# Weight operands of the second feed-forward half made during the first half and kept in DRAM

## The chip, the cores and the metric

The kernel runs on one core of one Trainium2 chip. The time is device microseconds of one execution. TensorE (PE) does the matmuls, VectorE (DVE), ScalarE (ACT) and GpSimd (POOL) the rest, SyncE (SP) issues most DMAs; POOL issues some of its own. SBUF is on the chip, PSUM holds what TensorE accumulates, DRAM is outside.

## The reference, cut to what matters

An encoder block on x (1024 tokens x 1024 columns, float32): attention with a pooling branch, a norm, and a feed-forward network whose hidden width is 2816. Only the last part is touched:

```python
h = modulate(layer_norm(x), sh2, sc2)
gt, up = jnp.split(h @ w_ffn_in[l], 2, axis=-1)
y = (jax.nn.silu(gt) * up) @ w_ffn_out[l]
x = layer_norm(ALPHA * x + g2[:, None, :] * y, ln2_g[l], ln2_b[l])
```

## The kernel before

Float32 products are made of three matmuls. `split` turns an operand into a high half (`hi`, a cast on ACT) and a low half (`lo` = operand - `hi`, a subtract on DVE), and `mm3` (lines 98 to 101) adds high x high, high x low and low x high in PSUM. Both halves of the feed-forward network are 2x2 block products in Winograd's form: seven products of blocks in place of eight, whose operands are blocks or sums and differences of blocks.

The **first half** (lines 1164 to 1179) runs over 22 pairs of column tiles (gate and up). A pair is seven products of 12 matmuls, 84 in all, into the PSUM tiles `fa` and `fb`. For each pair SP loads `rg` and `ru` (512 KB each); `rest_w` forms the sums of weights (POOL lines 973 and 979, DVE lines 975 and 980) and splits them into `oh`, `ol`. Between the products stand copies out of PSUM: `first_cp` copies `p1`, `rest_a` copies `u2` and `p5` (ACT, lines 1058 and 1061); DVE adds at lines 933, 1068 and 1070; the activation follows (lines 1074 to 1076), and two tiles `th` of 128 x 512 are stored to `midD` in DRAM by SP. Products accumulate on the same PSUM tiles, so a copy has to be done before the next product on its tile starts; TensorE works on the other tile meanwhile. The order on each engine is that of a scheduler here, except for the first pairs.

The **second half** (lines 1182 to 1440) multiplies the hidden activations, read back from `midD` into the blocks `m11`, `m12`, `m21`, `m22` (11 tiles of 128 x 512 each; `m11` lies in the tile `mA`, `m21` in `mB`), with the blocks of `w_ffn_out`. The order of all engines is written out by hand. Products go in the order q = 2, 1, 5, 6, 3, 7, 4, each in 11 steps k, and a step is 12 matmuls into four PSUM tiles `oa` or `ob`. Ahead of step i the program text puts: `loads` of weights six steps ahead (SP, 512 KB for two steps, into the three buffers of `raw`), `sums` four steps ahead and `splits` three steps ahead. `sums` forms the sums of activations on POOL (lines 1234, 1237, 1241, 1244) and the sums of weights: `wx` (POOL line 1231, DVE line 1238), line 1245 on POOL, and `t4_sum` (POOL line 1338, for product 4, whose weights `t4_load` brings into `mB`). `splits` splits both operands of a step: the activations to `moh`, `mol` (four buffers), the weights to `wo` (buffers `whi`, `wlo`, two each). The last two steps of product 7 and the last four of product 4 (`late`) are run per PSUM tile at the product's end, so that the tiles finish one after the other.

Between the steps stand `hooks`: POOL's loads of blocks (`chunk`, line 1331), the loads of the residual x1 from `x1D`, `zl` and `zr` (DVE lines 1269 and 1270: the residual of the first four row tiles), `zn` and `zo` (ACT's norm and, by `gain_pool`, POOL lines 1284 and 1285: gain and bias of the output, then the store to the output), and `c22` (residual and statistics for the last four row tiles, DVE lines 1269, 1270, 1307). `evac` empties the PSUM tiles at the end of each product.

Of the kernel before, what the change touches and what calls it, by code (L numbers as in the profile page):

```python
# [9 lines left out]
F32 = mybir.dt.float32  # L10
# [8 lines left out]
P = 128  # L19
# [16 lines left out]
def encoder_block_kernel(  # L36
# [37 lines left out]
    midD = dram.tile([2, NF, P, HF], F32, tag="midD", name="midD")  # L74

# [85 lines left out]
    # mod columns: GEMV of rows [128 k x 1024] accumulated on DVE, reduced over partitions by PE  # L161
# [40 lines left out]
    batch = [("u", 3, 3072 + 3 * P), ("u", 2, 3072 + 2 * P), ("q", 0, 0)]  # L202
    wb = {}
    with tc.tile_pool(name="pre", bufs=1, reuse_waits="tile") as pre:
# [99 lines left out]
        def batch_mm(g0, n0=0, n1=6, step=1):  # L304
            """The first products with the contraction outermost, as the tiles of h arrive."""
# [21 lines left out]
        def distances(i):  # L327
            """Half of the table of -|key - query|."""
# [82 lines left out]
        # lambda  # L411
# [69 lines left out]
    with ExitStack() as ctx2:  # L481
# [39 lines left out]
        # ---- pooling branch, with the projections of head 0  # L521
# [191 lines left out]
        # remaining modulation vectors  # L713
# [243 lines left out]
    def rest_w(f, rawg, rawu, step):  # L957
        """Operands (gate, up columns) of the last five products of pair f: their sums and splits."""
# [224 lines left out]
    # Token halves, halves of the hidden channels and column halves form 2x2 blocks again;  # L1183
    # the sums of blocks replace blocks that no later product reads.
    mA = big.tile([P, 16, HF], F32, tag="A", name="mA")
    mB = big.tile([P, 16, HF], F32, tag="B", name="mB")
    with tc.tile_pool(name="fo", bufs=1, reuse_waits="tile") as fo:
# [5 lines left out]
        wx = fo.tile([P, NK, HF], F32, name="wx")  # L1193
# [12 lines left out]
        raws, ops, src = {}, {(2, k): out_ops[k] for k in range(2)}, {}  # L1206

        def wload(q, p, i, j):
            n = min(2, NK - p)
            r = wp.tile([P, 2, HF], F32, tag="raw", bufs=3, name="w%d_%d" % (q, p))  # L1210
            nc.sync.dma_start(r[:, 0:n, :], wblock(i, j, p, n))
            raws[q, p] = r[:, 0:n, :]

        WSRC = {2: (1, 0), 1: (0, 0), 6: (1, 1), 3: (1, 1), 7: (0, 0)}
# [255 lines left out]
```

## Time and profile before

| | |
|---|---|
| median of 3 runs | 1675.31 us (1674.59 to 1677.12) |
| span of the profiled execution (the only time given for it) | 1677.4 us |
| PE busy | 1578.5 us, 94% |
| DVE busy | 1189.5 us, 71% |
| ACT busy | 709.9 us, 42% |
| POOL busy | 421.7 us, 25% |
| DMA over the span | 190.76 MB, 114 GB/s |

The profile is of one execution, so a sum made from its rows gives a time against 1677.4 us; the median of the runs is 2.1 us below that. The feed-forward network's first half ends and its second half starts at about 1401 us; the last matmul ends near 1660.8 us, and the output's last tiles follow. Shares of the whole span say little about either half; the rows further down are of stretches of them.

### The profile page before, as it was taken

The page shows a single profiled execution, that of the slowest core. Times are in us where ns is not written, and L with a number is a line of the kernel's source. Part 1 is how long each engine was busy: PE and PEld are TensorE (multiplying, and loading weights), DVE is VectorE, ACT ScalarE, POOL GpSimd, SP SyncE. Part 2 cuts the span into 40 slices and gives each one's busy share as a digit, 9 for nine tenths or more (in the row PEclk, how much of TensorE's full clock was granted, in tenths as well). Part 3 has the DMA queues.
Part 4 walks back from the last instruction along what each step waited for, and adds up shares of the span by engine and source line. Part 5 has one row for each costly group of instructions (what it writes and reads, how often), then busy time and mean ns, then how long its engine had stood idle before and what let it go on. Part 6 is the DMA issues. An engine that isn't in the chain of part 4 may idle for free.

```text
span 1677.4 us, 20367 instructions
## 1 busy us (share of the span) xinstructions
PE 1578.5 (94%) x7634; PEld 1308.7 (78%) x7634; DVE 1189.5 (71%) x1664; ACT 709.9 (42%) x1228; POOL 421.7 (25%) x382
## 2 busy tenths in 40 slices
PE   5899999999999999999989979999999999969874
PEld 3787888888888888888878757888888888858653
DVE  7676868685966667675657896555555554898998
ACT  3445545454545545454532444333333334425341
POOL 4300001010102101000142471212111111574793
PEclk8999999999999999999999989999999999989997
DMA  9244334151433323213063513322322228724321
GB/s 332 60 122 145 105 95 132 45 150 64 133 94 101 120 82 119 57 57 101 27 224 131 170 51 100 97 80 78 99 76 86 77 89 290 255 76 150 107 107 63
DMA packets 169333, 190.76 MB, mean 114 GB/s; under 512 B 7185, under 2 KB 125010, under 8 KB 169234
## 3 DMA queue, kind: packets, MB, share of 16 engines
q1 hardware_dynamic: 165392, 176.06, 33.6%
q0 software_dynamic: 3184, 12.32, 2.0%
q8 instruction: 60, 0.98, 0.2%
q10 hardware_dynamic: 658, 1.08, 0.2%
q14 instruction: 39, 0.32, 0.1%
HBM read 144.34 MB, written 36.70 MB: 108 GB/s over the span
## 4 chain that ended last, share of the span: by engine, by line
PE 75%; DVE 14%; issue 4%; DMA 3%; POOL 3%; ACT 1%; SPq 0%; DVEq 0%; POOLq 0%; ACTq 0%
PE fa L99 4%; PE fa L100 4%; PE fa L101 4%; PE fb L99 3%; PE fb L100 3%; PE fb L101 3%; PE at L651 3%; PE s L628 3%; PE s L630 3%; DVE wo L96 2%; PE pp L99 2%; PE pp L100 2%; PE pp L101 2%; PE pv L99 2%; PE pv L100 2%
## 5 line engine op out<-in xcount | busy, mean ns | idle before, releaser
L637 ACT ACTIVATE e<-e,nm 128x1024 f32<-128x1024 f32 x128 | 147.1, 1150 | 111.1 <-DVE nm L635 109.8
L635 DVE CUSTOM_DVE_ANT_0 e<-s,table 128x1024 f32<-128x1024 f32 x128 | 153.1, 1217 | 24.9 <-PE s L630 24.4
L96 DVE TENSOR_TENSOR ol<-ws,oh 128x512 fp32r<-128x512 f32 x88 | 61.0, 695 | 76.4 <-ACT oh L95 76.3
L628 PE MATMUL s<-k,q 128*128 128x512 f32 x256 | 105.3, 411 | 1.2 <-DVE nm L635 1.2
L96 DVE TENSOR_TENSOR al<-at,ah 128x512 fp32r<-128x512 f32 x128 | 83.2, 684 | 31.9 <-ACT ah L95 31.4
L979 POOL TENSOR_TENSOR ws<-rg,ru 128x512 f32<-128x512 f32 x22 | 45.7, 2075 | 228.1 <-DVE ol L96 217.2
L630 PE MATMUL s<-k,q 128*128 128x512 f32 x256 | 101.5, 397 | 0.0
L95 ACT CAST oh<-ws 128x512 fp32r<-128x512 f32 x88 | 53.9, 616 | 104.4 <-POOL ws L979 66.7
L642 DVE SCALAR_TENSOR_TENSOR e<-e,c,e 128x1024 f32<-128x1024 f32 x64 | 87.4, 1365 | 1.9
L100 PE MATMUL oa<-wo,moh 128*128 128x512 f32 x176 | 73.0, 415 | 15.3 <-DVE wo L96 15.3
L95 ACT CAST ah<-at 128x512 fp32r<-128x512 f32 x128 | 70.0, 596 | 25.1 <-PE at L651 25.1
L99 PE MATMUL oa<-wo,moh 128*128 128x512 f32 x176 | 71.6, 407 | 3.3 <-ACT wo L95 3.3
L651 PE MATMUL at<-ident,e 128*128 128x128 f32 x512 | 68.9, 275 | 6.0 <-DVE e L642 3.2
L99 PE MATMUL av<-ah,vh 128*128 128x256 f32 x256 | 73.9, 289 | 0.3 <-ACT ah L95 0.2
L99 PE MATMUL fa<-oA,oh 128*128 128x512 f32 x176 | 69.8, 397 | 2.9 <-ACT oh L95 2.7
L101 PE MATMUL av<-ah,vl 128*128 128x256 f32 x256 | 72.6, 284 | 0.0
L100 PE MATMUL av<-al,vh 128*128 128x256 f32 x256 | 72.5, 283 | 0.0
L101 PE MATMUL oa<-wo,mol 128*128 128x512 f32 x176 | 71.9, 408 | 0.0
L101 PE MATMUL fa<-oA,ol 128*128 128x512 f32 x176 | 69.7, 396 | 1.1 <-DVE ol L96 1.0
L100 PE MATMUL fa<-oA,oh 128*128 128x512 f32 x176 | 69.6, 396 | 0.5 <-DVE oA L1051 0.5
L681 POOL TENSOR_TENSOR rm_1v<-rm_1s,rm_1v 128x4 f32<-128x4 f32 x8 | 5.0, 624 | 251.8 <-ACT rm_1s L672 251.8
L651 PEld LDWEIGHTS at<-ident,e 128*128 128x128 f32 x512 | 58.7, 144 | 11.7 <-DVE e L642 3.6
(562 smaller groups left out, 4812.3 us busy)
## 6 DMA issues: line engine op xcount, KB each, us to landing
ada<-in_w_ada_dram SPq DMA_DIRECT2D x32, 512.0 KB, 3.8
rg<-in_w_ffn_in_dram SPq DMA_DIRECT2D x26, 512.0 KB, 3.9
w<-in_w_ffn_out_dram SPq DMA_DIRECT2D x24, 512.0 KB, 3.9
ru<-in_w_ffn_in_dram SPq DMA_DIRECT2D x22, 512.0 KB, 3.8
midD<-th SPq DMA_DIRECT2D x42, 256.0 KB, 2.1
q<-q SPq DMA_DIRECT2D x32, 256.0 KB, 2.9
mt<-mixD SPq DMA_DIRECT2D x12, 448.0 KB, 6.4
x<-in_x_dram SPq DMA_DIRECT2D x8, 512.0 KB, 6.3
```

The costliest lines, as they stand in the source:

```text
L95: nc.scalar.copy(hi, src)
L96: (eng or nc.vector).tensor_tensor(lo, src, hi.bitcast(F32), op=ALU.subtract)
L99: nc.tensor.matmul(ps, lh, rh, start=start, stop=False, skip_group_check=skip)
L100: nc.tensor.matmul(ps, lh, rl, start=False, stop=False, skip_group_check=skip)
L101: nc.tensor.matmul(ps, ll, rh, start=False, stop=stop, skip_group_check=skip)
L628: nc.tensor.matmul(ps[:, cs], q[:, 0, jj * P:(jj + 1) * P], kd[h, m][:, cs], start=True, stop=False)
L630: nc.tensor.matmul(ps[:, cs], q[:, 1, jj * P:(jj + 1) * P], kd[h, m][:, cs], start=False, stop=True)
L635: nc.vector.tensor_tensor_reduce(out=t, in0=ps, in1=table[:, o0:o0 + S], scale=-slope, scalar=3.0e38, op0=ALU.add, op1=ALU.min, accum_out=nm)
L637: nc.scalar.activation(t, t, AF.Exp, bias=nm, scale=-1.0, accum_out=zt[:, m, j:j + 1])
L642: nc.vector.scalar_tensor_tensor(s[1], s[1], c1, s[0], op0=ALU.mult, op1=ALU.add)
L651: nc.tensor.matmul(pt[:, i, :], a[:, kt * P:(kt + 1) * P], ident, start=True, stop=True, is_transpose=True)
L979: pol(sa, r11, r21, op=ALU.subtract)
```

## The change

A new DRAM tile `wfD` holds, for each of the seven products and each k, a finished weight operand: both halves of a tile, 128 partitions x 2 x 512, 512 KB, 4 KB in a row per partition.

`fw_prep`, a generator, makes them in the first half. For each k it loads the four blocks of `w_ffn_out` (256 KB each, one buffer each), splits the seven operands into tiles `fwo` (two buffers; ACT's cast, DVE's subtract), stores each with a DMA on SP, and forms the sums between by four POOL subtractions. The loop over pairs draws eight pieces of it for every k, spread over the pairs from the second on. In all: 44 loads, 77 casts, 77 subtracts on DVE, 44 on POOL, 77 stores.

In the second half the weights' loads, sums and splits go, and so do `wx`, `t4_load` and `t4_sum`. `fw_load` reads a step's operand from `wfD` into a ring of seven buffers (the ones that `raw`, `whi` and `wlo` had), still six steps ahead. At the end of products 7 and 4 the loads, like the splits, now stand behind the late blocks. TensorE's rows are the same 6817 in the same order.

```diff
+    RING = ("whi", "wlo", "raw", "whi", "wlo", "raw", "raw")
+    def fw_load(q, k):
+        tag = RING[nring[0] % len(RING)]
+        nring[0] += 1
+        w = wp.tile([P, 2, HF], F32R, tag=tag, bufs=3 if tag == "raw" else 2, name="w%d_%d" % (q, k))
+        nc.sync.dma_start(w.bitcast(F32), wfD[q - 1, k])
+        return w
...
+    def fw_prep():
+        def op(q, k, src):
+            w = fwp.tile([P, 2, HF], F32R, tag="fwo", bufs=2, name="fw%d_%d" % (q, k))
+            split(w[:, 0, :], w[:, 1, :], src)
+            nc.sync.dma_start(wfD[q - 1, k], w.bitcast(F32))
+        for k in range(NK):
+            w11, w12, w21, w22 = [fwp.tile([P, HF], F32, tag="fw%d%d" % ij, bufs=1, name="fw%d%d_%d" % (*ij, k))
+                                  for ij in ((0, 0), (0, 1), (1, 0), (1, 1))]
...
+            op(2, k, w21)
+            pol(w12, w12, w11, op=ALU.subtract)
+            yield
+            op(3, k, w22)
+            pol(w22, w22, w12, op=ALU.subtract)
+            yield
+            op(1, k, w11)
+            pol(w11, w22, w11, op=ALU.subtract)
...
+            op(5, k, w12)
+            pol(w21, w21, w22, op=ALU.subtract)
...
         if f == 0:
             hrs.close()
+            fwp = hp.enter_context(tc.tile_pool(name="fwp", bufs=1, side="right", reuse_waits="tile"))
+            prep = fw_prep()
+        else:
+            for _ in range(8 * NK * f // (NF - 2) - 8 * NK * (f - 1) // (NF - 2)):
+                next(prep, None)
...
         def loads(q, k):
-            if k % 2 == 0 and q in WSRC:
-                wload(q, k, *WSRC[q])
+            ws[q, k] = fw_load(q, k)
...
             elif q == 1:
-                pol(x, x, w, op=ALU.subtract)
-                r = m11_, w
+                r = m11_
...
             split(m[0], m[1], src[q, k][0])
-            split(w[:, 0, :], w[:, 1, :], src[q, k][1])
-            ops[q, k] = (m, w)
+            ops[q, k] = (m, ws[q, k])
...
-                        if fn is splits and n and k == NK - 1:
-                            behind.append(steps[i + ahead])
+                        if fn is not sums and n and k == NK - 1:
+                            behind.append((fn, steps[i + ahead]))
```

ACT in the first half, pair 12, from the cast of its fourth operand to the copy `p5`. Before:

```order
L95 CAST oh12_3_10239<-ws12_1_10222 128x512
L928 COPY p1_12_10218<-fa12_10192 128x512
L1074 ACTIVATE th12_0_10313<-p1_12_10218 128x512
L95 CAST oh12_4_10243<-ru12_10186 128x512
L1058 COPY u2_12_10259<-fa12_10192 128x512
L95 CAST oh13_0_10364<-ws13_1_10361 128x512
L1061 COPY p5_12_10273<-fb12_10193 128x512
```

Now; `fw<q>_<k>` is the operand of product q, step k, and `fw00` to `fw11` are the four blocks:

```order
L96 CAST oh12_3_10483<-ws12_1_10466 128x512
L96 CAST fw2_8_11072<-fw10_8_11066 128x512
L96 CAST fw3_8_11216<-fw11_8_11067 128x512
L929 COPY p1_12_10462<-fa12_10436 128x512
L96 CAST fw1_8_11221<-fw00_8_11064 128x512
L1075 ACTIVATE th12_0_10557<-p1_12_10462 128x512
L96 CAST fw5_8_11226<-fw01_8_11065 128x512
L96 CAST oh12_4_10487<-ru12_10430 128x512
L1059 COPY u2_12_10503<-fa12_10436 128x512
L96 CAST fw6_8_11231<-fw11_8_11067 128x512
L1062 COPY p5_12_10517<-fb12_10437 128x512
```

The scheduler put five casts of `fw_prep` among these rows, two directly ahead of the copy `p1` and one directly ahead of `p5`; over the whole half it packs `fw_prep` into pairs 1 to 15 and leaves pairs 16 to 21 without.

POOL at the start of the second half, from its first load there (`m12`, `mA`, `mB`, `m22` are the blocks of activations). Before:

```order
L1331 DMA m12_11601<-midD_76 128x512
L1331 DMA mA_11596<-midD_76 128x4x512
L1416 DMA wx_11604<-in_w_ffn_out_dram 128x4x512
L1331 DMA mA_11596<-midD_76 128x7x512
L1416 DMA wx_11604<-in_w_ffn_out_dram 128x7x512
L1231 TENSOR_TENSOR wx_11604<-wx_11604,w1_0_11744 128x1024
L1231 TENSOR_TENSOR wx_11604<-wx_11604,w1_2_11784 128x1024
L1231 TENSOR_TENSOR wx_11604<-wx_11604,w1_4_11825 128x1024
L1331 DMA mB_11597<-midD_76 128x4x512
L1331 DMA m22_11605<-midD_76 128x4x512
L1231 TENSOR_TENSOR wx_11604<-wx_11604,w1_6_11870 128x1024
L1231 TENSOR_TENSOR wx_11604<-wx_11604,w1_8_11913 128x1024
```

Now:

```order
L1359 DMA m12_12042<-midD_76 128x512
L1359 DMA mA_12037<-midD_76 128x4x512
L1359 DMA mA_12037<-midD_76 128x7x512
L1359 DMA mB_12038<-midD_76 128x4x512
L1359 DMA m22_12045<-midD_76 128x4x512
L1359 DMA mB_12038<-midD_76 128x7x512
L1359 DMA m22_12045<-midD_76 128x7x512
L1269 TENSOR_TENSOR mB_12038<-mB_12038,m22_12045 128x1024 x5
L1269 TENSOR_TENSOR mB_12038<-mB_12038,m22_12045 128x512
```

The loads of `wx` and its sums (line 1231) are gone, and with them what stood between the loads: seven loads of activations follow one another.

DVE in product 4, from the split of step 4 to that of step 5, with one `c22` between. Before:

```order
L96 TENSOR_TENSOR mol4_4_13150<-m22_11605,moh4_4_13149 128x512
L96 TENSOR_TENSOR wo4_4_13151<-mB_11597,wo4_4_13151 128x512
L1269 TENSOR_TENSOR m12_11601<-m12_11601,mA_11596 128x512
L1270 SCALAR_TENSOR_TENSOR m12_11601<-mA_11596,m12_11601 128x512
L1307 BN_STATS e3_11603<-m12_11601 128x6
L96 TENSOR_TENSOR mol4_5_13172<-m22_11605,moh4_5_13171 128x512
L96 TENSOR_TENSOR wo4_5_13173<-mB_11597,wo4_5_13173 128x512
```

Now:

```order
L97 TENSOR_TENSOR mol4_4_13439<-m22_12045,moh4_4_13438 128x512
L1297 TENSOR_TENSOR m12_12042<-m12_12042,mA_12037 128x512
L1298 SCALAR_TENSOR_TENSOR m12_12042<-mA_12037,m12_12042 128x512
L1335 BN_STATS e3_12044<-m12_12042 128x6
L97 TENSOR_TENSOR mol4_5_13460<-m22_12045,moh4_5_13459 128x512
```

The subtract for the weights (`wo`) is gone from each step; that of the activations (`mol`) and the three rows of `c22` stay.

## Rows read from the trace of the kernel before

**Rows 1.** Windows: busy us (and instructions) by engine, granted clock, DMA

```profile
core 0: us, PE busy (x) PEld busy (x) DVE busy (x) ACT busy (x) POOL busy (x), PEclk, DMA share, GB/s
1067.00:1401.00 334.00, 333.91 (x1473) 276.49 (x1474) 181.55 (x263) 118.39 (x196) 57.32 (x33) 1.00 0.29 93
...
1474.00:1510.00 36.00, 23.05 (x86) 17.86 (x85) 35.86 (x27) 8.23 (x16) 24.22 (x10) 0.86 0.28 89
...
1548.00:1599.60 51.60, 45.30 (x191) 36.29 (x189) 48.55 (x45) 16.43 (x28) 39.22 (x20) 0.97 0.37 117
1599.60:1660.80 61.20, 47.48 (x170) 35.39 (x168) 57.29 (x66) 19.47 (x31) 38.03 (x30) 0.89 0.19 70
```

**Rows 2.** TensorE's waits in the second half: us in total, times, longest

```profile
PE oa L100 <- DVE wo L96: 15.3, 8, 4.9
PE ob L100 <- DVE wo L96: 14.4, 4, 8.0
...
PE oa L99 <- ACT wo L95: 3.3, 2, 2.1
```

**Rows 3.** Timeline of POOL: start us, us, engine, line, operation

```profile
1474.31 15.56 POOL L1237 TENSOR_TENSOR mA<-mB,mA 128x1024 f32<-128x1024 f32 x6
```

**Rows 4.** Timeline of DVE: in A, at B's dense stretch, in C

```profile
1485.91 2.82 DVE L96 TENSOR_TENSOR wo<-wx,wo 128x512 fp32r<-128x512 f32 x1
...
1576.69 2.47 DVE L1378 TENSOR_TENSOR zlo<-zlo,ob 128x512 f32<-128x512 f32 x4
...
1617.08 2.88 DVE L96 TENSOR_TENSOR wo<-mB,wo 128x512 fp32r<-128x512 f32 x1
...
1650.05 0.68 DVE L96 TENSOR_TENSOR wo<-mB,wo 128x512 fp32r<-128x512 f32 x1
```

**Rows 5.** Groups, second half: busy us, mean ns | idle before, releaser

```profile
L96 DVE TENSOR_TENSOR wo<-w,wo 128x512 fp32r<-128x512 f32 x42 | 47.3, 1127 | 1.5 <-ACT wo L95 1.2
...
L1338 POOL TENSOR_TENSOR mB<-mB,wx 128x512 f32<-128x512 f32 x11 | 18.3, 1678 | 34.6 <-DMA mB<-in_w_ffn_out_dram 34.6
...
L1245 POOL TENSOR_TENSOR w<-wx,w 128x1024 f32<-128x1024 f32 (+1 forms) x6 | 14.5, 2410 | 6.8 <-DMA w<-in_w_ffn_out_dram 6.8
...
L1231 POOL TENSOR_TENSOR wx<-wx,w 128x1024 f32<-128x1024 f32 (+1 forms) x6 | 13.7, 2296 | 23.5 <-DMA w<-in_w_ffn_out_dram 23.5
...
L1284 POOL TENSOR_TENSOR zlo<-zlo,mA 128x1024 f32<-128x1024 f32 x4 | 10.9, 2728 | 0.0
L1285 POOL TENSOR_TENSOR zlo<-zlo,mB 128x1024 f32<-128x1024 f32 x4 | 10.8, 2702 | 0.3
```

**Rows 6.** Groups, first half, 1067 to 1401: same columns

```profile
L96 DVE TENSOR_TENSOR ol<-ws,oh 128x512 fp32r<-128x512 f32 x68 | 46.9, 690 | 63.1 <-ACT oh L95 63.1
L95 ACT CAST oh<-ws 128x512 fp32r<-128x512 f32 x68 | 41.9, 616 | 81.2 <-POOL ws L979 51.1 <-PE fb L100 27.3 <-PE fa L100 2.8
...
L973 POOL TENSOR_TENSOR ws<-ru 128x512 f32<-128x512 f32 x16 | 20.7, 1291 | 63.3 <-DVE ol L96 39.4 <-DMA ru<-in_w_ffn_in_dram 23.9
...
L1068 DVE TENSOR_TENSOR p<-p,fa 128x512 f32<-128x512 f32 x18 | 12.4, 688 | 16.8 <-PE fa L101 16.8
...
L1058 ACT COPY u<-fa 128x512 f32<-128x512 f32 x18 | 10.4, 579 | 0.0
```

**Rows 7.** DMA from 1412 to 1424: packets, MB, share; us to landing

```profile
DMA packets 1403, 4.64 MB, mean 386 GB/s; under 512 B 80, under 2 KB 80, under 8 KB 1402
...
q0 software_dynamic: 986, 3.84, 83.9%
q1 hardware_dynamic: 416, 0.79, 18.1%
...
w<-in_w_ffn_out_dram SPq DMA_DIRECT2D x3, 512.0 KB, 9.1
```

**Rows 8.** DMA issues of the whole run: KB each, us to landing

```profile
x1D<-zx SPq DMA_DIRECT2D x4, 512.0 KB, 2.6
```

More of the change, by code (lines that the diff above doesn't have):

```diff
@@ L1144, in encoder_block_kernel @@
     NK = NF // 2
-    def wblock(i, j, p, n):
-        return wfo[(i * NK + p) * P:(i * NK + p + n) * P, j * HF:(j + 1) * HF].rearrange("(f p) c -> p f c", p=P)
+    RING = ("whi", "wlo", "raw", "whi", "wlo", "raw", "raw")
+    nring = [0]
+    def fw_load(q, k):
[4 more added lines that the diff above has]
+        return w
     def first_out():
-        m, w = [wp.tile([P, 2, HF], F32, tag="raw", bufs=3, name="raw_" + nm) for nm in ("m", "w")]
+        ws = [fw_load(2, k) for k in range(2)]
+        m = wp.tile([P, 2, HF], F32, tag="raw", bufs=3, name="raw_m")
+        nring[0] += 1
         nc.sync.dma_start(m, midD[0, NK:NK + 2].rearrange("f p c -> p f c"))
-        nc.sync.dma_start(w, wblock(1, 0, 0, 2))
         ops = []
@@ L1157, in first_out @@
                   for tag in ("oh", "ol")]
-            wo_ = wp.tile([P, 2, HF], F32R, tag=("whi", "wlo")[k], bufs=2, name="w_%d" % k)
             split(mo[0], mo[1], m[:, k, :])
-            split(wo_[:, 0, :], wo_[:, 1, :], w[:, k, :])
-            ops.append((mo, wo_))
-        return ops
+            ops.append((mo, ws[k]))
+        return ops
+    def fw_prep():
[6 more added lines that the diff above has]
+                                  for ij in ((0, 0), (0, 1), (1, 0), (1, 1))]
+            for w, i, j in ((w11, 0, 0), (w12, 0, 1), (w21, 1, 0), (w22, 1, 1)):
+                nc.sync.dma_start(w, wfo[(i * NK + k) * P:(i * NK + k + 1) * P, j * HF:(j + 1) * HF])
+            yield
[4 more added lines that the diff above has]
+            pol(w22, w22, w12, op=ALU.subtract)
+            yield
+            op(1, k, w11)
+            pol(w11, w22, w11, op=ALU.subtract)
+            yield
+            op(5, k, w12)
+            pol(w21, w21, w22, op=ALU.subtract)
+            yield
+            op(6, k, w22)
+            yield
+            op(7, k, w11)
+            yield
+            op(4, k, w21)
+            yield
     for f in range(NF):
@@ L1204, in encoder_block_kernel @@
             b += [s_[:, 0:HF], s_[:, HF:]]
[L1206 to L1214, printed above, removed]
+        ops, src = {(2, k): out_ops[k] for k in range(2)}, {}
+        ws = {}
         def loads(q, k):
-            if k % 2 == 0 and q in WSRC:
-                wload(q, k, *WSRC[q])
+            ws[q, k] = fw_load(q, k)
         def sums(q, k):
@@ L1224, in sums @@
             n = min(2, NK - k)
[L1225 to L1227 removed]
+            m11_, m12_, m21_, m22_ = [m[:, k:k + n, :] for m in (m11, m12, m21, m22)]
             if q == 2:
[L1229 removed]
+                r = m12_
             elif q == 1:
[L1231 to L1232 removed]
+                r = m11_
             elif q == 5:
                 pol(m21_, m21_, m22_, op=ALU.add)
[L1235 removed]
+                r = m21_
             elif q == 6:
                 pol(m11_, m21_, m11_, op=ALU.subtract)
[L1238 to L1239 removed]
+                r = m11_
             elif q == 3:
                 pol(m12_, m12_, m11_, op=ALU.subtract)
[L1242 removed]
+                r = m12_
             elif q == 7:
                 pol(m11_, m22_, m11_, op=ALU.subtract)
[L1245 to L1246 removed]
+                r = m11_
             else:
[L1248 removed]
+                r = m22_
             for i in range(n):
[L1250 to L1252 removed]
+                src[q, k + i] = r[:, i, :]
         def splits(q, k):
@@ L1331, in chunk @@
             q.dma_start(dst[:, p:e, :], midD[half, k0 + p:k0 + e].rearrange("f p c -> p f c"))
-        def t4_load():
-            for p, e in ((0, 4), (4, NK)):
-                nc.sync.dma_start(m21[:, p:e, :], wblock(1, 0, p, e - p))
-        def t4_sum(k):
-            pol(m21[:, k, :], m21[:, k, :], wx[:, k, :], op=ALU.subtract)
         xh = [xr[:, 0:HF], xr[:, HF:]]
@@ L1362, in encoder_block_kernel @@
             hook(*((7, 9), (4, 0), (4, 2), (4, 4))[t], zo, t)
-        hook(6, NK - 1, t4_load)
-        for k in range(NK):
-            hook(3, k, t4_sum, k)
         def evac(q, t):
@@ L1415, in encoder_block_kernel @@
                 chunk(m11, 0, 0, p, e, nc.gpsimd)
-                nc.gpsimd.dma_start(wx[:, p:e, :], wblock(0, 1, p, e - p))
             for i in range(-6, len(steps)):
@@ L1438, in encoder_block_kernel @@
                         evac(q, t)
-                    for step in behind:
-                        splits(*step)
+                    for fn, step in behind:
+                        fn(*step)
 _INS = ['x', 'c', 'w_ada', 'b_ada', 'w_in', 'lambda_q1', 'lambda_k1', 'lambda_q2', 'lambda_k2', 'sub_g',
```

19 lines of the change are left out of this document (2 added, 17 removed).

## The prediction

> **What bounds the kernel now.** The table of windows comes first [rows 1], since the two halves of the feed-forward network have different limits. In the first half TensorE is never idle: 1473 matmuls in 334.00 us, 0.2267 us each, clock 1.00, VectorE (DVE) busy for 181.55 us of the 334. There only TensorE sets the time. The second half needs 7 x 132 = 924 matmuls, 209.5 us at that rate, and takes 258.97 us (1401.80 to 1660.77): 49 us are lost. By the same rows, length less matmuls x 0.2267:
> A, 1474 to 1510: 36.0 - 86 x 0.2267 = 16.5 us. B, 1548 to 1599.6: 51.6 - 191 x 0.2267 = 8.3 us. C, 1599.6 to 1660.8: 61.2 - 170 x 0.2267 = 22.7 us. In A and C the granted clock is below 1 (0.86, 0.89), so part of the loss is matmuls that ran slower after a gap.
>
> The list of TensorE's waits tells for whom it waits: 15.3 + 14.4 us for the low half of a weight operand (`wo`, DVE), 3.3 us for its high half [rows 2]. The timelines of GpSimd (POOL) and DVE tell why that is late: in A POOL runs sums without a pause, six of 1024 columns in 15.56 us [rows 3], and in that time one DVE subtract of 512 columns with both operands in SBUF takes 2.82 us [rows 4], against 0.69 us on average in the first half [rows 6]. With four operations of 2.47 us together (0.62 each) DVE reading PSUM is spared at such a time [rows 4]. So while POOL is dense, DVE does about one subtract per 2.8 us. A step of TensorE (12 matmuls) lasts 2.72 us and now asks for two subtracts, one for the activations, one for the weights: 5.6 us. That is the loss.
>
> **What the change takes out of the second half.** 77 casts on ScalarE (ACT), 77 `wo` subtracts on DVE (42 of them are the first of [rows 5]), six more sums on DVE, and on POOL the sums of weights: 18.3 + 14.5 + 13.7 = 46.5 us [rows 5]. TensorE's work and order stay. One subtract per step is left: 2.8 us against 2.72 at POOL's densest, about even.
>
> A: what could remain is the residuals of product 5 (two DVE operations every second step), if POOL is still dense there: nine operations x 2.8 = 25 us in five steps (13.6 us), less three steps of operands in hand (8 us), 3 us. From 0 (POOL done earlier: its activations load sooner) to 8 us. I take 2: **gain 14.5 us**.
>
> B: the stretch has 39.22 us of POOL work in 51.6 us; without the sums of line 1338 and most of line 1245, no dense run covers two steps. I leave 1 of 8.3 (0.5 to 3): **gain 7.3 us**.
>
> C: the end is set by the last `wo` at 1650.05 [rows 4], behind which the sixteen late blocks of product 4 run (48 matmuls, 10.9 us, to 1661). DVE's queue to that point passes POOL's run of the output gain, 10.9 + 10.8 = 21.7 us [rows 5], which stays, and which leaves DVE eight places of 2.8 us whatever stands in them. Nine `wo` fewer (11 in product 4, two done before the run) shorten the queue behind the run by 9 x 0.65 = 5.9 us. The 3.3 us of waits for the high half [rows 2] stand just before the run; they go, but SP's queue holds the x1 loads of the residuals behind operand loads now, so I count 2.5 of them. Bounds: 3 us (only those waits), 13 us (product 4 at 132 x 0.2267 = 29.9 us from its start at 1617). **Gain 8.4 us.**
>
> **What it adds at the seam.** The start of the second half now puts all loads of the POOL queue in a row: 33 blocks of 256 KB for the hidden activations and one in advance, 8.9 MB with no sum between. Before, such loads drew 3.84 MB in 12 us, 320 GB/s, while SP's queue got 0.79 MB, 66 GB/s, and a weight load of 512 KB took 9.1 us to land [rows 7]. At 320 GB/s 8.9 MB take 28 us, 10.3 steps. Each step needs 512 KB; five are in hand (loads run six steps ahead), and 66 GB/s x 28 us brings 3.5 more: 8.5 of 10.3, so 1.8 steps, 5 us, are lost. The other end is zero. SP's packets there were 0.79 MB / 416 = 1.9 KB; the finished pairs are read in rows of 4 KB. If SP's queue keeps its count of packets it gets 132 GB/s, 7 loads, and nothing is late. I take the measured rate: **loss 5 us**, since that row is of the same two queues.
>
> The Trainium skill, page "DMA: Bandwidth & Descriptors", section "Queues, rings and completion order", says that each DMA engine turns between the queues that have work, a packet from each. By that the two queues would share some 386 GB/s evenly, 193 GB/s for SP, just what a step of 2.72 us draws, and the sum would be 5 us better (R4 below). The counts (986 packets against 416 in this window) don't show an even turn, though nothing there says that SP's queue always had work.
>
> **What it adds to the first half.** 44 loads, 77 casts, 77 DVE subtracts, 44 POOL subtracts and 77 stores of 512 KB (40 MB), packed by the order into pairs 1 to 15: 5.1 operands a pair, whose length is 84 matmuls, 19.0 us. Per pair:
> DVE: 181.55 / 17.6 pairs = 10.3 us, plus 5.1 x 0.69 = 3.5, plus up to 2.9 POOL sums x 1.29 us [rows 6] during which DVE may stand, 3.8: 17.6 of 19.0. ACT: 118.39 / 17.6 = 6.7, plus 5.1 x 0.62 = 3.2: 9.9. DMA: 93 GB/s, plus 51 MB / 285 us = 179: 272 GB/s, under the 386 that a full window showed [rows 7]. Nothing is over its limit, so the bound from below is zero.
>
> But order costs. The new operand has two buffers, so a cast waits for the store two operands earlier. Such a turn is cast 0.62, subtract 0.69 [rows 6], some 0.4 to issue, and a landing of 2.6 us [rows 8] to 4 (my estimate beside other traffic): 4.3 to 5.7 us. 5.1 operands through two buffers take 11 to 14.5 us of 19. They fit, but not at any moment: ACT's order puts such casts directly ahead of the copies `p1`, `u2` and `p5`. The next product but one overwrites what they read, so each has a product of 2.72 us less its own 0.58 [rows 6], 2.1 us, to be late. The same holds of DVE's line 1068, which TensorE needs one product later and which now can meet a POOL sum. A cast that arrives a turn too early can stand 1 to 4 us, past that room. I take 0.6 us a pair, 15 pairs: **loss 9 us** (0 to 28, the end at 1.9 us a pair, one full late turn less the room).
>
> **Sum.** 14.5 + 7.3 + 8.4 - 5 - 9 = 16.2 us. The profiled execution's span is 1677.4 us; 1661.2 follows, and the median of the runs is 2.1 us below the span: **1659 us**.
>
> **Rivals.**
> R1, slower: the two-buffer ring bounds the first half. It decides when a turn passes 8.2 us, since 5.1 x 8.2 / 2 = 20.9 is a pair plus the room of 2.1 us. At 9 us a pair loses 4 us, 60 over fifteen, and the time is 1675.3 - (16.2 + 9) + 60 = 1710. For it: loads, which took 9.1 us in a full window [rows 7], and SP, one queue for the stores and the pair's own weight loads. Against: 272 GB/s is not full, and 512 KB stored landed in 2.6 us [rows 8]. Chance 0.14.
> R2: the first half's loss is about 25 us (1.7 us a pair, the waits of ACT and DVE adding up): it eats the gain, within 0.2%. 0.08.
> R3: A or the seam is worse: POOL's sums stay dense through product 5 (8 us left in place of 2), or the loads starve five steps (13 us): some 7 less, 1666. 0.14.
> R4: the seam's loads come in time (packets of twice the size): 1654. 0.12.
> R5: the first half hides all: 1650; with R4 also 1645. 0.15.
>
> **How the numbers follow.** My forecast's own chance is 0.37. Faster: 0.37 + 0.14 + 0.12 + 0.15 = 0.78; same 0.08; slower 0.14. A measurement of this kernel can tell some 0.2%, 3.4 us, from no change. The range leaves out R1 and a little of both ends: from 1641 (R4, R5 and 3 us more from C) to 1680 (R2 with a late turn more).
>
> **What would show it.** Right: the first half's window with a few idle us on TensorE in pairs 1 to 15, ended by ACT copies or DVE `p`, and none in 16 to 21; waits for `wo` gone from A and B, replaced in the first 30 us of the second half by short waits for DMA; DVE's 2.8 us subtracts still there, one a step. Wrong: idle times of TensorE over 2 us in every pair 1 to 15, with ACT standing for `fw` stores (R1); or long waits for `mol` in product 5 (R3). The term I trust least is the 9 us.

## The result and the profile after

The changed kernel takes 1699.45 us (median of 4 runs, 1697.01 to 1701.16) beside 1675.01 us of the kernel before: a ratio of 1.0142, interval 1.0128 to 1.0157. It is slower by some 24 us; 1659 us was forecast, with a range of 1641 to 1680. The profiled execution's span is 1696.6 us, against 1677.4.

The first thing to look at is where the second half starts. Its first matmul (the tile `ob`) stands at 1444.29 us in the timeline of TensorE, against 1401.80 before [rows 1]: the first half lost 42.5 us. From there to the end of the last matmul, 1679.3 us, are 235.0 us, against 258.97: the second half gained 24.0 us. What follows the last matmul is 17.3 against 16.6 us. 42.5 - 24.0 + 0.7 = 19.2 us is the difference of the spans.

Windows of the kernel after, columns as in [rows 1]: the stretch of pairs 2 to 15 or so, then the second half cut at its own slow places.

```profile
1000.00:1320.00 320.00, 286.25 (x1181) 225.62 (x1181) 246.03 (x308) 140.65 (x242) 117.80 (x76) 0.97 0.68 234
...
1444.30:1514.00 69.70, 69.70 (x313) 57.82 (x312) 30.61 (x32) 19.61 (x33) 29.44 (x18) 1.00 0.92 348
1514.00:1550.00 36.00, 30.29 (x123) 24.17 (x122) 31.56 (x20) 8.26 (x14) 28.46 (x12) 0.91 0.56 191
1550.00:1630.00 80.00, 80.00 (x355) 66.29 (x354) 32.01 (x49) 21.95 (x34) 13.81 (x16) 1.00 0.65 218
1630.00:1645.00 15.00, 8.92 (x31) 6.89 (x30) 8.13 (x11) 4.61 (x6) 6.56 (x7) 0.77 0.45 169
1645.00:1679.30 34.30, 29.29 (x119) 22.74 (x117) 32.21 (x32) 4.58 (x8) 21.18 (x13) 0.95 0.46 161
```

And the same 320 us of the kernel before:

```profile
1000.00:1320.00 320.00, 315.58 (x1375) 258.81 (x1374) 183.94 (x268) 116.17 (x196) 62.14 (x36) 0.99 0.28 86
```

In equal time TensorE did 1181 matmuls in place of 1375: 194 x 0.2267 = 44 us. Of these 29 are idle time (33.8 us against 4.4); the rest are matmuls that took longer, at a granted clock of 0.97 against 0.99. DVE was busy 246 of 320 us and POOL 118, nearly twice as much as before; no engine is full, and DMA moved 234 GB/s. TensorE's waits in that window (us in total, times, longest):

```profile
PE fa L100 <- ACT p L929: 14.7, 8, 3.8
PE fa L100 <- DVE p L1069: 8.0, 8, 2.9
PE fa L100 <- ACT u L1059: 5.9, 7, 2.0
PE fb L100 <- DVE p L934: 3.8, 3, 1.9
```

It waits for the copies and sums that clear PSUM, 20.6 us for those on ACT and 11.8 us for those on DVE; in the second half's list of before [rows 2] it waited for operands. One of these waits, on ACT, then on TensorE (start, us, operation, idle time ahead and what ended it):

```profile
1087.63 0.61 ACT L96 CAST oh<-ws 128x512 fp32r<-128x512 f32 x1
1092.31 0.62 ACT L96 CAST fw<-fw 128x512 fp32r<-128x512 f32 x1 [4.07 <-DMA wfD<-fw]
1092.84 0.58 ACT L929 COPY p<-fa 128x512 f32<-128x512 f32 x1
```

```profile
1093.47 0.50 PE L100 MATMUL fa<-oA,oh 128*128 128x512 f32 x1 [3.39 <-ACT p L929]
```

The cast of a new operand stands ahead of the copy `p1`, waits 4.07 us for a store to land, and TensorE, which needs the copy's PSUM tile, stands 3.39 us. In all ACT waited 63.2 us for such stores there, 32 times. And the groups of the first half, 1000 to 1310 us, as in [rows 6]:

```profile
L97 DVE TENSOR_TENSOR fw<-fw,fw 128x512 fp32r<-128x512 f32 x73 | 63.8, 885 | 26.0 <-ACT fw L96 25.7
L97 DVE TENSOR_TENSOR ol<-ws,oh 128x512 fp32r<-128x512 f32 x60 | 54.2, 906 | 14.9 <-ACT oh L96 13.4 <-PE fc L101 0.7 <-PE fa L101 0.3
...
L1197 POOL TENSOR_TENSOR fw<-fw,fw 128x512 f32<-128x512 f32 x11 | 18.0, 1639 | 0.9
```

DVE's subtract for a pair's own operand takes 906 ns on average, 690 before; the new ones 885; a POOL sum of weights 1.4 to 1.6 us, where 1.29 was counted.

### The profile page after: what moved, and what is told of

It is laid out like the page before. It is cut to its first block, busy times and chain, and to the rows that moved or that the text cites. A ratio compares the mean times of both kernels' runs of the same rounds, so it can differ in the third digit from the quotient of the medians.

```text
span 1696.6 us, 20752 instructions
## 1 busy us (share of the span) xinstructions
PE 1582.3 (93%) x7634; PEld 1307.8 (77%) x7634; DVE 1183.2 (70%) x1658; ACT 711.9 (42%) x1228; POOL 430.8 (25%) x401
## 4 chain that ended last, share of the span: by engine, by line
PE 67%; DVE 14%; DMA 8%; issue 5%; ACT 3%; POOL 3%; SPq 0%; DVEq 0%; ACTq 0%; POOLq 0%
DMA wfD<-fw 3%; PE at L652 3%; PE s L629 3%; PE s L631 3%; PE fa L100 2%; PE fa L102 2%; PE fa L101 2%; PE oa L102 2%; PE oa L100 2%; PE oa L101 2%; PE pp L100 2%; PE pp L101 2%; PE pp L102 2%; PE pv L100 2%; PE pv L101 2%
## 5 line engine op out<-in xcount | busy, mean ns | idle before, releaser
L97 DVE TENSOR_TENSOR ol<-ws,oh 128x512 fp32r<-128x512 f32 x88 | 75.3, 857 | 34.1 <-ACT oh L96 32.5
L100 PE MATMUL fa<-oA,oh 128*128 128x512 f32 x176 | 74.2, 422 | 23.3 <-ACT p L929 14.7
L96 ACT CAST fw<-fw 128x512 fp32r<-128x512 f32 x77 | 47.1, 619 | 91.5 <-DMA wfD<-fw 64.1
L97 DVE TENSOR_TENSOR fw<-fw,fw 128x512 fp32r<-128x512 f32 x77 | 66.5, 875 | 26.8 <-ACT fw L96 26.4
L100 PE MATMUL oa<-w,moh 128*128 128x512 f32 x176 | 70.2, 399 | 6.1 <-issue 6.1
L102 PE MATMUL oa<-w,mol 128*128 128x512 f32 x176 | 70.2, 399 | 5.0 <-DVE mol L97 5.0
L101 PE MATMUL fa<-oA,oh 128*128 128x512 f32 x176 | 72.5, 412 | 0.5 <-DVE oA L1052 0.5
L980 POOL TENSOR_TENSOR ws<-rg,ru 128x512 f32<-128x512 f32 x22 | 39.4, 1792 | 126.6 <-DVE ol L97 117.1
L101 PE MATMUL oa<-w,moh 128*128 128x512 f32 x176 | 70.0, 398 | 0.0
```

Of the source, the lines that this page charges most:

```text
L96: nc.scalar.copy(hi, src)
L97: (eng or nc.vector).tensor_tensor(lo, src, hi.bitcast(F32), op=ALU.subtract)
L100: nc.tensor.matmul(ps, lh, rh, start=start, stop=False, skip_group_check=skip)
L101: nc.tensor.matmul(ps, lh, rl, start=False, stop=False, skip_group_check=skip)
L102: nc.tensor.matmul(ps, ll, rh, start=False, stop=stop, skip_group_check=skip)
L980: pol(sa, r11, r21, op=ALU.subtract)
```

## Experiments

Each kernel's start of the second half is that of its first `ob` matmul in its profiled execution; two executions with the same first half gave 1444.3 and 1442.7. Ratios are to the kernel before.

**Which half loses.** The operands are made for k = 0 alone:

```diff
-        nc.sync.dma_start(w.bitcast(F32), wfD[q - 1, k])
+        nc.sync.dma_start(w.bitcast(F32), wfD[q - 1, 0])
...
-        for k in range(NK):
+        for k in range(1):
```

> Leaves out: the operands are made for k = 0 alone (7 in place of 77), and the second half reads those for every k, so its transfers, waits and matmuls are the changed kernel's. It parts the change's two halves. In the changed kernel the second half starts 42 us later than before (1444.3 against 1401.8 us) and is 24 us shorter. If the making of the operands is the cause of the 42 us, by whichever mechanism, this kernel's second half starts at 1400 to 1406 us, is as short as the changed kernel's (235 us from its first matmul to its last), and the time is 1650 to 1657 us. If something else in the changed program (the other loads at the seam, another order) costs the 42 us, the start stays above 1420 us and the time above 1670 us.

Start 1403.5 us, first to last matmul some 232 us, 1654.48 us (0.9888, 0.9867 to 0.9908). The making of the operands is the cause of the 42 us, and the second half alone is worth 19 us of time.

**Spread, and the ring's depth.** In `e7_even` a cast is an activation with a bias of zero made from its pair's `u2`, so that the order can't draw it into an earlier pair:

```diff
-            split(w[:, 0, :], w[:, 1, :], src)
+            nc.scalar.activation(w[:, 0, :], src, AF.Identity, bias=hold[1])
+            vec(w[:, 1, :], src, w[:, 0, :].bitcast(F32), op=ALU.subtract)
```

> The whole computation. The same 77 operands, but each cast is bound to its pair by a zero bias made from that pair's u2, so that pairs 2 to 21 hold 3 to 5 each in place of 5 to 7 in pairs 3 to 15. Theory RING (two buffers, a turn of about 8 us for two operands with the store's landing, and ACT's copies behind casts that wait): 3.6 operands a pair leave 10.5 us a turn, the 42 us fall under 12, time 1655 to 1670 us. Theory LOCK (each operand costs TensorE its 0.5 us wherever it stands, since POOL's sums and the extra subtracts crowd DVE): the sum over pairs stays 30 to 42 us, time 1687 to 1700 us. Theory TRAFFIC (the pair's own weight loads land later at 240 GB/s than at 93): 225 GB/s over more pairs, some 20 to 30 us stay, 1677 to 1687 us.

Start 1430.4 us, 1687.09 us (1.0076, 1.0054 to 1.0097): the 42.5 us fell only to 28.6. RING missed. The 28.6 us are in TRAFFIC's range of 20 to 30 and just under LOCK's of 30 to 42, and the time is where the two ranges meet, so this run doesn't part them.

Then two kernels without POOL's sums, with casts bound and 5 operands a pair, two source tiles, and either two or three buffers:

```diff
-            w = fwp.tile([P, 2, HF], F32R, tag="fwo", bufs=2, name="fw%d_%d" % (q, k))
+            w = fwp.tile([P, 2, HF], F32R, tag="fwo", bufs=3, name="fw%d_%d" % (q, k))
```

> Leaves out POOL's sums of weights in the first half (operands of products 4, 6, 7 and 5 are made from single blocks), so that two source tiles suffice; the ring of two buffers and 5 operands a pair in pairs 2 to 17 stay, as do 77 casts, 77 subtracts, 77 stores and 44 loads. It is the base for the run with three buffers. RING: 30 to 42 us of loss stay, time 1685 to 1700 us. LOCK: without POOL's sums the loss falls under 15 us, 1660 to 1672 us. TRAFFIC: as RING.

> The kernel with two source tiles and without POOL's sums, with one edit: the ring of finished operands has three buffers in place of two (its 4 KB per partition come from the two source tiles given up). RING: a cast waits for the store three operands earlier, 11 us in place of 7.5 for a turn, and the loss falls to 5 to 15 us: 20 us or more below the two-buffer run. LOCK and TRAFFIC: no difference to the two-buffer run beyond 5 us, since work and bytes are the same.

Two buffers: start 1411.0 us, 1666.15 us (0.9952, 0.9937 to 0.9968), the time that LOCK gave for a kernel without POOL's sums. Three: 1402.7 us, 1654.62 us (0.9891, 0.9868 to 0.9914). So the third buffer is worth 8 us of start and 11.5 us of time, less than RING said, more than the others did; and with neither sums nor a short ring, and casts bound, 77 casts, 77 subtracts and 40 MB of stores cost the first half 1 us. So traffic alone costs at most that 1 us, at 248 GB/s in the window, and TRAFFIC falls (with two buffers, then with three):

```profile
1000.00:1320.00 320.00, 306.67 (x1327) 248.93 (x1327) 235.20 (x334) 160.31 (x263) 63.84 (x52) 0.99 0.73 246
```

```profile
1000.00:1320.00 320.00, 311.37 (x1361) 254.02 (x1360) 238.81 (x338) 160.02 (x267) 67.29 (x52) 1.00 0.72 248
```

**The sums.** Leaving POOL's four sums a k out of the changed kernel, moving them to DVE (`pol` to `vec` in the same four lines), and putting equal but idle work back into the two-buffer kernel:

```diff
-            pol(w12, w12, w11, op=ALU.subtract)
+            vec(w12, w12, w11, op=ALU.subtract)
```

```diff
+                pol(dead[0], dead[0], dead[1], op=ALU.subtract)
```

> Leaves out POOL's 44 sums of weights in the first half (the operands of products 4 to 7 are made from single blocks); all else, two buffers, four source tiles, order and packing into pairs 3 to 15, is the changed kernel's. So far the second half starts at 1444.3 us in the changed kernel, at 1411.0 us without the sums and with two source tiles, at 1401.8 us before. If the sums alone carry that difference, the start is at 1408 to 1416 us and the time 1662 to 1672 us. If the other order of the operands or the source tiles of the earlier run carried it, the start stays at 1430 us or later, time over 1680 us.

> The whole computation: the changed kernel with its 44 sums of weights moved from POOL to DVE (0.69 us each, 30 us of DVE work more). Theory LOCK (while POOL works on two SBUF operands, DVE's subtracts stand): the sums cost DVE 0.69 us each in place of some 1.3 us of standing, and the start comes down to 1412 to 1422 us, time 1665 to 1675 us. Theory QUEUE (POOL's sums wait for loads and splits in POOL's one queue and hold back the pair's own sums, and behind those SP's loads): the same waits now stand in DVE's queue, which more wait for; the start stays at 1435 us or rises, time over 1688 us.

> The two-buffer kernel without sums (start 1411.0 us, 1666 us) with 44 POOL subtracts of the same size put back on two scratch tiles: they wait for nothing but their pair's u2, and nothing waits for them. LOCK: the work itself is what hurts; the start rises to 1425 us or more, time 1680 us or more. QUEUE: the work without the waits is free; start within 5 us of 1411, time 1663 to 1671 us.

Without: 1426.5 us, 1680.73 us (1.0031, 1.0017 to 1.0046), a start between the two that were forecast, so the sums carry 18 us but not the rest. On DVE: 1424.7 us, 1679.25 us (1.0025, 1.0011 to 1.0039): no dearer than none, and between the ranges of LOCK and QUEUE, nearer to LOCK's. On scratch tiles: 1449.6 us, 1702.93 us (1.0160, 1.0143 to 1.0177): 44 POOL subtracts for which nothing waits cost 38.6 us of start. In this run LOCK holds and QUEUE falls. The window of that kernel shows how: POOL at 126 us, DVE 251 in place of 235 us though it did fewer instructions, TensorE at 1180 matmuls.

```profile
1000.00:1320.00 320.00, 285.21 (x1180) 226.08 (x1178) 250.86 (x301) 143.34 (x236) 126.36 (x102) 0.97 0.65 220
```

From 1000 to 1450 us its longest waits are for `p` on DVE (11 times):

```profile
PE fb L100 <- DVE p L934: 22.2, 11, 3.2
```

The subtracts could also have held back the pair's own sums `ws` behind them in POOL's queue. They didn't: ACT's casts waited 29.5 us for line 980 from 1000 to 1320 us, against 33.4 us without them, and DVE 4.9 against 6.6 us for line 974. What grew is DVE's operations. In the same 320 us the subtract of a new operand (line 1182) averages 962 ns, against 730 without the idle subtracts. One run of three of them, and DVE's rows beside it:

```profile
1152.06 5.52 POOL L1192 TENSOR_TENSOR dead<-dead,dead 128x512 f32<-128x512 f32 x3
```

```profile
1152.95 1.78 DVE L1079 SCALAR_TENSOR_TENSOR th<-th,u 128x512 f32<-128x512 f32 x1
1154.65 1.77 DVE L1182 TENSOR_TENSOR fw<-fs,fw 128x512 fp32r<-128x512 f32 x1
1156.35 0.67 DVE L1080 SCALAR_TENSOR_TENSOR th<-th,fa 128x512 f32<-128x512 f32 x1
```

The two with both inputs in SBUF took 1.78 and 1.77 us, the one that reads the PSUM tile `fa` 0.67. The sum `p` (line 934) reads PSUM too and took 679 ns on average; it was late because of what stood ahead of it on DVE. The subtracts came two to four in a row, denser than in the changed kernel, so 38.6 us is no measure of the 18. The Trainium skill, page "SBUF — State Buffer", section "SBUF: two separate sides", says that VectorE and GpSimd share one pair of SBUF ports as an exclusive lock for a whole instruction, for VectorE operations with two SBUF inputs beside a GpSimd operation that reads SBUF. The trace agrees: 1.78 and 1.77 us against 0.67 in the rows above.

A form meant to keep the gain, three buffers and sums on DVE with two source tiles and five loads a k:

```diff
+            x, y = ld(0, 0, k, "fsa"), ld(0, 1, k, "fsb")
+            op(1, k, x)
+            vec(y, y, x, op=ALU.subtract)
+            op(5, k, y)
+            x = ld(1, 1, k, "fsa")
...
+            w = fwp.tile([P, 2, HF], F32R, tag="fwo", bufs=3, name="fw%d_%d" % (q, k))
```

> The whole computation in a form meant to keep the second half's gain: sums on DVE, two source tiles used in turn (block 11 loaded twice, five loads of 256 KB for each k), a ring of three buffers, casts bound to their pairs and spread evenly over pairs 2 to 21 (3 to 5 each). RING and LOCK together: the first half loses at most 6 us, start 1402 to 1408 us, time 1653 to 1662 us. If waits for the five serial loads of each k, or the 30 us of DVE sums, reach TensorE, the start is at 1415 us or later and the time above 1668 us.

Start 1429.0 us, 1691.88 us (1.0097, 1.0076 to 1.0117), 30 us above the range that was hoped for; the second branch of the expectation came true. ACT's casts now waited for loads in series, and an operand reached the second half late (TensorE stood 7.1 us for it):

```profile
ACT fw L1181 <- DMA fsb<-in_w_ffn_out_dram: 17.1, 7, 5.5
ACT fw L1181 <- DMA fsa<-in_w_ffn_out_dram: 13.9, 9, 2.7
```

**What is left without sums: binding or order.** Four kernels with casts bound, 5 to 6 operands a pair, two buffers, four source tiles; they differ in where the sums run and in the order of a k's operands.

> The whole computation: sums on DVE as in the run with its start at 1424.7 us, and besides each cast bound to its pair as in the evenly spread run, but drawn for fifteen pairs, so that pairs 3 to 17 hold 5 to 6 operands each. Without sums, one kernel starts its second half at 1426.5 us (casts unbound, four source tiles) and another at 1411.0 us (casts bound, two source tiles, operands block by block). If the binding is the difference (unbound casts stand earlier in ACT's queue than their buffer comes free, and ACT's copies of PSUM wait behind them), the start comes to 1407 to 1415 us, time 1660 to 1669 us. If the two source tiles and the order by blocks are, the start stays at 1420 to 1428 us, time 1674 to 1683 us.

> Leaves out the sums of weights in the first half (operands are made from single blocks). Two buffers, four source tiles, casts bound to pairs, 5 to 6 operands a pair, the operands of a k in the changed kernel's order (2, 3, 1, 5, 6, 7, 4), in which block 21 is read by the first operand of a k and by the last, so that its next load can start only when the k is done. Base for the next run. Theory ORDER: start near the unbound kernel without sums, 1422 to 1428 us, time 1674 to 1682 us. If binding alone made the 1411.0 of the two-source kernel: 1409 to 1414 us, time 1663 to 1668 us.

> As the run before, with one edit: the operands of a k are made block by block (2, 4, 3, 6, 1, 7, 5), so that each source tile comes free after its second operand and its next load starts while the others are worked on. ORDER: 10 us or more below the run before, start at 1406 to 1414 us. If the rest of the loss is the ring's and the traffic's alone, no change (within 4 us).

> The whole computation: sums on DVE, casts bound, 5 to 6 operands a pair, as in the run whose start was 1422.7 us (time 1675.1 us), with one edit: the order of a k's operands is 1, 5, 3, 6, 7, 2, 4, in which no block is needed by both the first and the last. ORDER: start at 1408 to 1416 us, time 1661 to 1669 us. Otherwise 1420 to 1426 us.

> The whole computation: the changed kernel (sums on POOL, two buffers, four source tiles) with one edit: each cast is bound to its pair and the draws are for fifteen pairs, so that the operands per pair stay at 5 to 6. If ACT's casts that stand too early make a part of the loss on their own (19 us, as without sums), the start falls from 1444.3 to 1423 to 1428 us, time 1675 to 1681 us. If with POOL's sums the crowding of DVE and POOL sets the pace, binding gains as little as with sums on DVE: start 1438 to 1445 us, time 1692 to 1700 us.

Their edits to the changed kernel, beside the bound cast above, are the draws, the engine of the sums, and the lines of `fw_prep` put in another order:

```diff
-            for _ in range(8 * NK * f // (NF - 2) - 8 * NK * (f - 1) // (NF - 2)):
+            for _ in range(8 * NK * f // 15 - 8 * NK * (f - 1) // 15):
```

Start of the second half, us (median time in brackets; before: 1401.8):

| sums of weights | casts as the order packs them | casts bound to pairs, nearly as many a pair |
|---|---|---|
| none | 1426.5 (1680.73) | 1407.1 (1662.69) |
| on DVE | 1424.7 (1679.25) | 1422.7 (1675.08) |
| on POOL | 1444.3 (1699.45) | 1438.3 (1690.65) |

TensorE's idle time from 1000 to 1400 us in the same kernels, us, for the copies on ACT and for the sums on DVE that clear PSUM (before: 0.2 and 3.1):

| sums of weights | casts as the order packs them | casts bound to pairs |
|---|---|---|
| none | ACT 16.0, DVE 4.0 | ACT 5.2, DVE 3.5 |
| on DVE | ACT 9.2, DVE 11.7 | ACT 6.1, DVE 12.8 |
| on POOL | ACT 20.6, DVE 11.8 | ACT 11.6, DVE 19.1 |

Binding alone took the start to 1407.1 us without sums, 2 us past the second branch of that expectation, and little with sums on POOL. With sums on DVE the start stayed in the range that was given to source tiles and order; that reason fell with the next runs. The order of operands is not the cause: block by block gave 1415.1 us (1666.80 us; 0.9944, 0.9927 to 0.9960) against 1407.1 (0.9923, 0.9909 to 0.9938), and with sums on DVE 1422.2 (1675.80 us; 1.0004, 0.9991 to 1.0018) against 1422.7 (0.9999, 0.9990 to 1.0009). ORDER falls; `d0_dense` is 1.0074 (1.0051 to 1.0097). Read by rows, binding takes 19 us where nothing else crowds DVE, and 2 to 6 us where sums do; with POOL's sums the start is that of the slowest of five executions, and the medians put it at 9 us. ACT's waits for stores fall with it, from 59.4 to 28.9 us without sums and from 63.2 to 23.7 us with POOL's. Read by columns, POOL's sums cost 18 and 31 us. The causes overlap: whichever is taken away first, the other still holds part of the time. The idle times tell the same by engine: binding frees ACT's copies (16.0 to 5.2 us), sums delay DVE's (3.5 to 12.8 or 19.1 us), and with POOL's sums binding moves a part of the wait from ACT to DVE:

```profile
PE fb L100 <- DVE p L934: 13.6, 8, 3.3
PE fa L100 <- DVE p L1072: 5.5, 6, 2.9
PE fa L100 <- ACT p L929: 4.4, 3, 1.9
```

These are rows of `d0_dense`, 1000 to 1400 us.

**The second half's own waits.** One edit: the residuals take the x1 tiles loaded ahead.

```diff
-            residual(zlo[:, t, hi_], zlo[:, t, hi_], hi_, x1load(t, hi_, xr[:, t % 2 * HF:t % 2 * HF + HF]))
+            residual(zlo[:, t, hi_], zlo[:, t, hi_], hi_, xh[t % 2])
```

> The whole computation: the changed kernel with one edit in the second half: the residuals of the first four row tiles use the x1 tiles that were loaded ahead, and don't load them a second time. In the changed kernel DVE stands 6.3 us at 1630 us for the second load of x1 of row tile 3, which SP issued behind six other x1 loads and operand loads, and TensorE stands 6.1 us right behind. If that load is the cause, these waits go and the second half is 5 to 9 us shorter (226 to 230 us), time 1690 to 1695 us, with the first half as it was. If TensorE there waited for its own operands from DRAM, nothing changes (within 3 us).

Start 1442.7, first to last matmul 225.4 us in place of 235.0, 1689.75 us (1.0085, 1.0070 to 1.0100), a little more than the 5 to 9 us expected. The load was the cause. In the changed kernel DVE stood for it here:

```profile
1636.10 0.69 DVE L1298 SCALAR_TENSOR_TENSOR zlo<-mB,zlo 128x512 f32<-128x512 f32 x1 [6.33 <-DMA mB<-x1D]
```

**Fewer operands.** Only products 5, 6, 7 and 4, which need sums, get operands from the first half; products 2, 1 and 3 split single blocks in the second half as before. Sums on DVE, casts bound and spread.

```diff
+            vec(w12, w12, w11, op=ALU.subtract)
+            op(5, k, w12)
+            vec(w22, w22, w12, op=ALU.subtract)
+            op(6, k, w22)
+            vec(w11, w22, w11, op=ALU.subtract)
+            op(7, k, w11)
+            vec(w21, w21, w22, op=ALU.subtract)
+            op(4, k, w21)
...
+            if q in WSRC:
+                w = wp.tile([P, 2, HF], F32R, tag=("whi", "wlo")[cnt[0] % 2], bufs=2, name="wo" + nm)
+                split(w[:, 0, :], w[:, 1, :], raws[q, k])
```

> The whole computation, with operands made in the first half for products 5, 6, 7 and 4 alone (44 in place of 77, the four that need sums; sums on DVE, casts bound to pairs, 2 to 3 a pair). Products 2, 1 and 3 load and split single blocks in the second half as before. If the first half's loss goes with the operands a pair must take past its two buffers, 2.2 a pair leave 17 us a turn and the start is at 1402 to 1408 us; if each operand has a price of its own (23 us / 77 = 0.3 us with sums on DVE), it is at 1415 us. Second half: stretches A, B and C lie in products 5 to 4, so 240 to 246 us from first to last matmul. Time 1655 to 1664 us in the first case, 1666 to 1674 us in the second.

> The whole computation: the mixed kernel with the x1 loads made once. If the x1 loads hold DVE there as in the changed kernel, 3 to 9 us below the mixed kernel; if its fewer operand loads had already let them through, within 2 us of it. A version that beats both kernels is expected here: 1650 to 1662 us.

> The whole computation: the mixed kernel with 44 operands and x1 loaded once (start 1406.3 us, time 1651.6 us), with one edit: the casts are not bound, so that the order packs them into pairs 3 to 11, 5 to 6 a pair, as the changed kernel's are. If density and casts ahead of the copies cost TensorE about 0.3 us an operand as with all 77 and sums on DVE, the start is at 1412 to 1418 us and the time 1657 to 1664 us; if fewer operands are cheap wherever they stand, within 2 us of 1651.6 us.

> The whole computation: that order, casts spread evenly over pairs 2 to 21 (3 to 5 operands a pair), sums on DVE, and x1 loaded once in the second half (worth 10 us there in the changed kernel, 235.0 to 225.0 us). By the sum of what the runs gave: first half 3 to 10 us lost, second half 225 us, start 1405 to 1412 us, time 1648 to 1657 us. If the spread brings the making of the last operands too near the second half, TensorE waits for operands from DRAM at its start, and the time is above 1660 us.

Mixed: start 1405.0, 1658.23 us (0.9901, 0.9884 to 0.9917), in the first case's range; its second half took 233.3 us from first to last matmul, less than the 240 to 246 expected. With x1 loaded once: 1406.3 us, 1651.61 us (0.9859, 0.9844 to 0.9874), **faster than both kernels**, by 23 us and 48 us. Without binding, the order packs its 44 operands into pairs 3 to 11: 1416.2 us, 1660.60 us (0.9906, 0.9891 to 0.9921), 10 us of start more, in the range that a price of 0.3 us an operand gave; so that price goes with where and how densely the operands stand. All 77 operands with sums on DVE, casts bound and spread, x1 once: 1416.0 us, 1662.48 us (0.9921, 0.9906 to 0.9935), above its range. The second half was 227 us and TensorE has no wait at its start, so the branch that named late operands has the time but not the reason: the first half lost 14 us, with 7.8 us of waits for DVE's `p` (line 934). The window of the best one has DVE as busy as others, yet 1353 matmuls:

```profile
1000.00:1320.00 320.00, 311.70 (x1353) 253.85 (x1353) 237.51 (x332) 133.09 (x224) 63.83 (x52) 0.99 0.52 172
```

## Why the prediction was wrong, step by step

- **What bounded the second half: right.** The `wo` waits of [rows 2] are gone, and matmuls run without a gap where the stretch is not one of those below.
- **A, gain 14.5: 8.4 measured.** 1514 to 1550 us: 36.0 - 123 x 0.2267 = 8.1 us remain, the end of the range. The 2 us that were left for it went by loads that come sooner. POOL's activations landed late again and its sums were dense through product 5, 15.35 and 15.59 us for two sets of six, as in R3; TensorE stood for `mol`:

```profile
1479.17 5.20 POOL L1269 TENSOR_TENSOR mB<-mB,m 128x1024 f32<-128x1024 f32 x2 [24.62 <-DMA m<-midD]
1496.78 9.71 POOL L1269 TENSOR_TENSOR mB<-mB,m 128x1024 f32<-128x1024 f32 x4 [12.42 <-DMA m<-midD]
1506.45 15.35 POOL L1272 TENSOR_TENSOR mA<-mB,mA 128x1024 f32<-128x1024 f32 x6
1521.76 15.59 POOL L1275 TENSOR_TENSOR m<-m,mA 128x1024 f32<-128x1024 f32 x6
1533.49 0.80 PE L102 MATMUL ob<-w,mol 128*128 128x512 f32 x1 [5.29 <-DVE mol L97]
```

- **B, gain 7.3: 8.3**, all of it; 1550 to 1630 us has no idle time on TensorE.
- **C, gain 8.4: 7.4.** What remains is 15 - 31 x 0.2267 = 8.0 us for the x1 load, which the prediction saw in SP's queue but priced at 0.8 us, and 34.3 - 119 x 0.2267 = 7.3 us in POOL's run of the output gain.
- **The seam, loss 5: nothing.** 1444.3 to 1514 us has 313 matmuls in 69.7 us, no loss. From 1450 to 1475 us SP's queue got 4.30 MB, 172 GB/s, not the 66 of [rows 7]; R4 was right on the seam. DMA in that window (queue: packets, MB, share):

```profile
q0 software_dynamic: 1292, 5.03, 55.7%
q1 hardware_dynamic: 1183, 4.30, 43.4%
```

The Trainium skill, page "DMA: Bandwidth & Descriptors", section "Queues, rings and completion order", has the engines turn between queues a packet at a time. The 1292 against 1183 packets of this profile agree with it, if they stand in the same ratio as the page's; the window doesn't show that both queues had work all the time, and why the count of [rows 7] was uneven stays open. Sum of the second half: 24.0 us gained where 25.2 were forecast. That the two are so near is in part luck: A fell short by 6 us and the seam was too dear by 5.

- **The first half, loss 9 (0 to 28): 42.5.** This is the step that failed. The prediction named a cast that waits for its store ahead of ACT's copies, and that is in the trace; but it priced it at 0.6 us a pair, and 42.5 / 15 = 2.8 were lost. Its turn of a buffer, 4.3 to 5.7 us, was too short: in the changed kernel the 33 casts that waited for a store began 7.1 us on average after the cast before last (3.6 to 10.7). And it took POOL's sums mainly as busy time, 17.6 of 19.0 us with nothing over its limit; that a PSUM sum can meet one was named, but only inside the 0.6 us. The runs show three causes in its place: POOL's sums, which stretch DVE's operations and so delay the PSUM sums and the new operands behind them (18 us, 31 with casts bound); casts that the order puts too early into ACT's queue (19 us without sums, 6 with POOL's); and the two-buffer ring (8 us without sums and with casts bound). With none of the three the start is 1402.7 us.
- **R1** had the sign and the mechanism in part, at chance 0.14, and its 1710 us is closer than the forecast. But its turn of over 8.2 us isn't the rule (7.1 us on average), and spread alone, which frees the ring, left 28.6 us of 42.5: that its number is near is luck in part.

**Open.** Why sums on DVE cost 15.6 us with bound casts (1407.1 to 1422.7) and none with unbound ones is only half settled: the idle times show that they add 8 to 9 us of waits for DVE in both, and that with unbound casts 7 us of waits for ACT go, but not why those go. How the 42.5 us divide while all three causes are present isn't settled either. Binding also thins the casts a little, from some 5.7 to 5.2 a pair, and no run parts the two. No kernel had a ring of three with the sums and four source tiles.

## What to carry to other kernels

That the engines' busy times fit doesn't make work free that is moved under a stretch where TensorE never waits. What counted here is the few us of room that each step which clears PSUM has, and what may now stand ahead of it in its engine's queue or slow the engine it runs on. In this kernel a POOL operation beside DVE took time from DVE, and DVE did the added sums for less than POOL. And move only what pays: here 44 of 77 operands, bound to their pairs, with x1 loaded once, brought the second half to 225.7 us and cost the first half 4.5 us.

## What the runs showed of the hardware

44 POOL subtracts of 128 x 512, on tiles that nothing else used, lengthened the first half by 38.6 us, 0.88 us each: that is more than half of their own mean of 1.59 us. And 40 MB of stores and 11.5 MB of loads beside the first half, 248 GB/s in the window, with a ring of three and no sums, cost 1 us. Beside a run of the idle POOL subtracts, DVE's operations with two inputs in SBUF took 1.78 and 1.77 us, and one that reads PSUM 0.67.
